# Two MLPs of a decoder trunk: one block fewer in seven products, sums moved later, transposes in two PSUM pools

## The chip, the cores and the metric

The kernel runs on one core of one Trainium2 chip. The metric is the device time in microseconds (us) of one execution, the median over several runs. One execution was also profiled; all rows below are of that one. TensorE multiplies (PE in the rows, PEld its weight loads), VectorE (DVE) and ScalarE (ACT) prepare its operands, and SyncE (SP) issues the loads.

## The reference, cut to what matters

Two residual layers over 256 tokens of width 2048, in float32: a differential attention layer, then a Mamba-2 layer, each followed by the same dense MLP with hidden width 8192:

```
def sq_relu_mlp(h, w1, w2):
    return jnp.square(jax.nn.relu(h @ w1)) @ w2
...
h = h + sq_relu_mlp(rms_norm(h, mlp_norm[i]), mlp_w1[i], mlp_w2[i])
```

The change touches only `h @ w1` and the squared ReLU after it, in both layers.

## The kernel before

Every matrix product is made from float32 numbers split in two parts: `split_weights` has ACT copy a 128x1024 piece of weights to the rounded high part (line 158) and then DVE subtract to get the low part (line 159). TensorE computes high by high, high by low and low by high. The weights come by DMA into 5 buffers (`raw`), the split pieces stand in 4 (`w`).

The hidden width is cut into eight blocks of 1024 (0 to 7), with the kinds in `MLP_KINDS`. A block of kind `s` ("plain") is `blocks`: eight groups of 128 columns, each in two steps of 8 k-tiles. One step (`wide_steps`) takes one piece of weights, 8 matmuls of 512 columns (line 169) and 8 of 256 (line 173), so a plain block has 16 steps and 16 pieces. `add_sums` (line 222) closes each group.

A block of kind `S` is `seven`: Strassen's scheme in its Winograd form over 2x2 quarters, with seven products P1 to P7 instead of eight. Each product is accumulated over four steps (i = 0 to 3); one step (`product`, lines 557 and 559) is 6 matmuls of 512 columns on one split piece of weights. That is 28 steps and 28 split pieces, and 16 additions of weights on DVE (lines 569, 579, 584, 600) that make the pieces which are sums of quarters. Seven sums of 128x512 on DVE (lines 587 to 591, 603 and 604, two copies on ACT) put the products together into the block's output `u`, and ACT applies ReLU and the square. `u` then stands tokens first, so `expand` transposes it on TensorE, 16 times 128x128 in four groups of four (line 656), and `split_pair` splits each group (ACT line 263, DVE line 264) into the operands `act` for the second matrix.

The second matrix is worked in four quarters q = 0 to 3, each of 32 token steps (`token_steps`, 12 matmuls of 512 columns on one split piece, lines 238 and 240). While quarter q runs, `both(q + 1)` makes blocks 2q+2 and 2q+3, and is advanced by `rate` steps per token step. So an MLP is: a first stage in which block 0 and block 1 alternate; q = 0 with blocks 2, 3; q = 1 with blocks 4, 5; q = 2 with blocks 6, 7; q = 3 with token steps alone. At the start of each quarter `expand` is queued for the two blocks just made (`side.add`); side work moves on by one `yield` at each `side.tick()`.

PSUM has three pools: `aux` (3 buffers: products of `seven`, and transposes), `aux1` (1: the product `p3`), and `mm` through `bank()` (4: token steps take two, a plain step's group one). Instructions of an engine run in the order in which a scheduler put them when the program was built; TensorE's is not exactly the order of the code.

Of the kernel before, what the change touches and what calls it, by code (L numbers as in the profile page):

```python
# [34 lines left out]
MASKED = -1.0e30  # L35


MLP_KINDS = "sSSSSSSS"


C_MIX0, C_MLP0, C_MIX1, C_MLP1 = 0, 16, 32, 48
# [50 lines left out]
def trunk_kernel(ctx: ExitStack, tc: tile.TileContext, x, xt, par, rope, qk, wv, wo, w10, w10s, w20, win, wdt, wout, w11, w11s, w21, out):  # L92
# [25 lines left out]
    def aux():  # L118
        return ps.tile([P, 512], F32, tag="aux", bufs=3, name="aux")
# [427 lines left out]
    def seven(pool, src, sas, u):  # L547


        a = [None] * 4  # L550

        def product(pp, which, w, i):
            for j, wj in enumerate(w):
                for kp in range(2):
                    ah, al = sas[2 * i + kp][which]
                    m = wj[:, kp * NB:(kp + 1) * NB]
                    PE.matmul(pp, lhsT=ah, rhs=m, start=(i + kp + j == 0), stop=(i == 3 and kp + j == 2))  # L557
                    if j == 0:
                        PE.matmul(pp, lhsT=al, rhs=m, start=False, stop=False)  # L559

        A11, S4, A12, S1, S3, S2, A22 = range(7)
        p1, p5 = aux(), aux()
        for i in range(4):
            while len(sas) < 2 * i + 2:
                side.tick()
            b11, b12 = load(src[0, i]), load(src[1, i])
            a[i] = pool.tile([P, 1024], F32, tag="wsum", bufs=4, name="wsum")
            w = split_weights(b11)
            V.tensor_tensor(out=a[i], in0=b11, in1=b12, op=ALU.subtract)  # L569
            product(p1, A11, w, i)  # L570
            yield
            product(p5, S1, split_weights(a[i]), i)
            yield
        S.copy(out=u[:, 0, 0], in_=p1)
        S.copy(out=u[:, 1, 1], in_=p5)
        p7, p3, p6 = aux(), aux1(), aux()
        for i in range(4):
            b12, b22 = load(src[1, i]), load(src[2, i])
            V.tensor_tensor(out=b12, in0=b22, in1=b12, op=ALU.subtract)  # L579
            product(p7, S3, split_weights(b12), i)  # L580
            yield
            product(p3, S4, split_weights(b22), i)
            yield
            V.tensor_tensor(out=a[i], in0=b22, in1=a[i], op=ALU.add)
            product(p6, S2, split_weights(a[i]), i)
            yield
        V.tensor_tensor(out=u[:, 0, 1], in0=p6, in1=u[:, 0, 0], op=ALU.add)
        V.tensor_tensor(out=u[:, 1, 0], in0=p7, in1=u[:, 0, 1], op=ALU.add)
        V.tensor_tensor(out=u[:, 0, 1], in0=u[:, 0, 1], in1=u[:, 1, 1], op=ALU.subtract)
        V.tensor_tensor(out=u[:, 0, 1], in0=p3, in1=u[:, 0, 1], op=ALU.add)  # L590
        V.tensor_tensor(out=u[:, 1, 1], in0=u[:, 1, 0], in1=u[:, 1, 1], op=ALU.subtract)
        for t in range(2):
            S.activation(u[:, t, 1], u[:, t, 1], AF.Relu)
            S.activation(u[:, t, 1], u[:, t, 1], AF.Square)
        p2, p4 = aux(), aux()
        for i in range(4):
            b21 = load(src[3, i])
            product(p2, A12, split_weights(b21), i)
            yield
            V.tensor_tensor(out=a[i], in0=a[i], in1=b21, op=ALU.subtract)  # L600
            product(p4, A22, split_weights(a[i]), i)
            yield
        V.tensor_tensor(out=u[:, 0, 0], in0=p2, in1=u[:, 0, 0], op=ALU.add)
        V.tensor_tensor(out=u[:, 1, 0], in0=u[:, 1, 0], in1=p4, op=ALU.subtract)
        for t in range(2):
            S.activation(u[:, t, 0], u[:, t, 0], AF.Relu)
            S.activation(u[:, t, 0], u[:, t, 0], AF.Square)
        yield

    def mlp(xs, w1, w1s, w2, pool, after):  # L610
# [29 lines left out]
        def expand(c, hid, place=None):  # L640
# [8 lines left out]
            for j in range(0, 4, 2):  # L649
                axs = []  # L650
                for i in range(2):
                    ax = aux().rearrange("p (a b) -> p a b", a=2)
                    for f in range(2):
                        for t in range(2):
                            c = T * (j + i) + P * f
                            PE.transpose(ax[:, f, t * P:(t + 1) * P], uf[:, t, c:c + P], ident)
                    axs.append(ax)
                for ax in axs:
                    hid += split_pair(ax, place)
                    yield  # L660

        def both(q, share):

            if not share:
                yield from hidden(2 * q)
# [7 lines left out]
            for _ in a:  # L673
                due += share
                yield
                while due >= 1:
                    due -= 1
                    next(b, None)
                    yield
            yield from b  # L680

        last = None
        side.add(sums_of(), slow=True)
        for _ in both(0, 28 / 12 if kinds[:2] == "sS" else 1.0):
            pass
        norm_mean()
        V.reciprocal(out=r2, in_=ms)
        for q in range(4):
            if q < 3:
                hid = []  # L690
                for c in (2 * q, 2 * q + 1):
                    side.add(expand(c, hid))
            else:
                hid = last
# [382 lines left out]
```

## Time and profile before

| | us |
|---|---|
| median of 3 runs | 2449.77 (2448.08 to 2452.68) |
| the profiled execution, its own time | 2449.62 |
| its span in the profile | 2447.9 |
| TensorE busy | 2434.1 |
| VectorE busy | 2098.2 |
| ScalarE busy | 1535.6 |

The span is the time from the first to the last instruction of the trace; 1.7 us of the execution lie around it. A matmul's row shows its duration with its latency, and the next one starts before it ends. So what a matmul costs is read from the starts of the rows, and a wait of TensorE is a start that comes later than the start before it plus that cost.

### The profile page before, as it was taken

To read this page: it belongs to the slowest core of one execution; us is meant where nothing else is said; L and a number is where in the kernel's file an instruction comes from. 1 tells how busy PE (TensorE), PEld (TensorE's weight loads), DVE (VectorE), ACT (ScalarE), POOL (GpSimd) and SP (SyncE) were. 2 spreads that over 40 slices of the span, in tenths; PEclk is the share of its full clock that TensorE was granted. 3 is DMA by queue.
4 is the path that set the end of the run, shared out by engine and by line. 5 is a ranking of instruction groups with operands and counts; after the bars stand their busy time and mean duration, and the time that the engine had idled before them with its cause. 6 is when DMAs were issued, how large, how long until landed. Compare 5 with 4: busy or idle time off the path is not lost.

```text
span 2447.9 us, 32626 instructions
## 1 busy us (share of the span) xinstructions
PE 2434.1 (99%) x12050; PEld 2038.8 (83%) x12050; DVE 2098.2 (86%) x2591; ACT 1535.6 (63%) x2154; POOL 1.2 (0%) x8
## 2 busy tenths in 40 slices
PE   9999999999999999999999999999999999999999
PEld 8888888878888788888888888888887888878887
DVE  6988879999998999568886887887899999899964
ACT  7666656666666666456776575775666666666653
POOL 0000000000000000000000000000000000000000
PEclk9999999999999999999999999999999999999999
DMA  8545555667667676556565556556566766776764
GB/s 287 164 157 175 167 175 194 208 232 243 230 208 230 221 231 218 191 177 211 190 198 196 174 198 199 166 189 191 190 218 220 239 229 203 238 232 206 233 205 147
DMA packets 140192, 500.54 MB, mean 204 GB/s; under 512 B 15648, under 2 KB 15840, under 8 KB 140032
## 3 DMA queue, kind: packets, MB, share of 16 engines
q1 hardware_dynamic: 137312, 489.75, 61.3%
q10 hardware_dynamic: 2720, 8.71, 1.0%
q8 instruction: 94, 1.54, 0.2%
q14 instruction: 66, 0.54, 0.1%
HBM read 496.24 MB, written 2.16 MB: 204 GB/s over the span
## 4 chain that ended last, share of the span: by engine, by line
PE 70%; DVE 18%; DMA 7%; issue 4%; ACT 1%; DVEq 0%; SPq 0%; ACTq 0%
PE pp L238 21%; PE pp L169 16%; DVE w L159 11%; PE pp L240 10%; PE pp L173 9%; PE aux L557 6%; DMA raw<-in_w11s 3%; DMA raw<-in_w10s 3%; PE aux L559 3%; DVE wsum L569 1%; DVE wsum L600 1%; DVE raw L579 1%; PE aux L878 1%; DVE h L716 1%; ACT w L158 1%
## 5 line engine op out<-in xcount | busy, mean ns | idle before, releaser
L159 DVE TENSOR_TENSOR w<-raw,w 128x1024 fp32r<-128x1024 f32 x858 | 1034.6, 1219 | 196.1 <-ACT w L158 193.5
L158 ACT CAST w<-raw 128x1024 fp32r<-128x1024 f32 x858 | 892.7, 1052 | 493.4 <-PE pp L238 316.3
L238 PE MATMUL pp<-w,act 128*128 128x512 f32 x3072 | 983.1, 391 | 0.7 <-ACT w L158 0.7
L238 PEld LDWEIGHTS pp<-w,act 128*128 128x128 f32 x3072 | 575.4, 188 | 121.7 <-ACT w L158 1.5
L240 PE MATMUL pp<-w,act 128*128 128x512 f32 x1536 | 598.5, 390 | 0.0
L169 PE MATMUL pp<-act,w 128*128 128x512 f32 x2000 | 489.0, 392 | 0.0
L169 PEld LDWEIGHTS pp<-act,w 128*128 128x128 f32 x2000 | 366.4, 188 | 72.6 <-issue 1.0
L240 PEld LDWEIGHTS pp<-w,act 128*128 128x128 f32 x1536 | 288.3, 188 | 58.0
L557 PE MATMUL aux<-w,sa 128*128 128x512 f32 x896 | 300.3, 392 | 5.2 <-DVE act L264 1.7
L173 PEld LDWEIGHTS pp<-act,w 128*128 128x128 f32 x2000 | 258.3, 191 | 11.0 <-issue 0.9
L173 PE MATMUL pp<-act,w 128*128 128x256 f32 x2000 | 266.8, 284 | 0.0
L158 ACT CAST w<-wsum 128x1024 fp32r<-128x1024 f32 x168 | 176.9, 1053 | 114.6 <-PE pp L238 43.8
L557 PE MATMUL aux<-w,act 128*128 128x512 f32 x672 | 228.8, 394 | 0.8 <-ACT w L158 0.3
L159 DVE TENSOR_TENSOR w<-wsum,w 128x1024 fp32r<-128x1024 f32 x168 | 204.8, 1219 | 1.9 <-ACT w L158 1.5
L557 PEld LDWEIGHTS aux<-w,sa 128*128 128x128 f32 x896 | 167.4, 188 | 44.3 <-DVE w L159 4.7
L559 PE MATMUL aux<-w,sa 128*128 128x512 f32 x448 | 175.2, 391 | 0.0
L557 PEld LDWEIGHTS aux<-w,act 128*128 128x128 f32 x672 | 124.8, 188 | 32.2 <-DVE w L159 6.2
L559 PE MATMUL aux<-w,act 128*128 128x512 f32 x336 | 131.4, 391 | 0.0
L559 PEld LDWEIGHTS aux<-w,sa 128*128 128x128 f32 x448 | 84.2, 188 | 16.7
L569 DVE TENSOR_TENSOR wsum<-raw 128x1024 f32<-128x1024 f32 x56 | 68.4, 1222 | 21.4 <-DMA raw<-in_w10s 11.5
L579 DVE TENSOR_TENSOR raw<-raw 128x1024 f32<-128x1024 f32 x56 | 68.5, 1222 | 20.4 <-DMA raw<-in_w11s 11.4
L600 DVE TENSOR_TENSOR wsum<-wsum,raw 128x1024 f32<-128x1024 f32 x56 | 68.0, 1220 | 7.4 <-DMA raw<-in_w11s 3.9
(218 smaller groups left out, 1736.0 us busy)
## 6 DMA issues: line engine op xcount, KB each, us to landing
raw<-in_w SPq DMA_DIRECT2D x288, 512.0 KB, 4.4
raw<-in_win SPq DMA_DIRECT2D x160, 512.0 KB, 4.1
raw<-in_w10s SPq DMA_DIRECT2D x140, 512.0 KB, 4.3
raw<-in_w11s SPq DMA_DIRECT2D x140, 512.0 KB, 4.3
raw<-in_wout SPq DMA_DIRECT2D x64, 512.0 KB, 4.1
raw<-in_qk SPq DMA_DIRECT2D x56, 512.0 KB, 4.3
raw<-in_wv SPq DMA_DIRECT2D x32, 512.0 KB, 4.2
raw<-in_wo SPq DMA_DIRECT2D x32, 512.0 KB, 4.2
```

Of the source, the lines that this page charges most:

```text
L158: S.copy(out=wh[:, s], in_=raw[:, s])
L159: V.tensor_tensor(out=wl[:, s], in0=raw[:, s], in1=wh[:, s].bitcast(F32), op=ALU.subtract)
L169: PE.matmul(acc, lhsT=wk, rhs=acts[k0 + k], start=(start and k == 0), stop=False)
L173: PE.matmul(acc[:, 0, :], lhsT=wk, rhs=acts[k0 + k][:, 0, :], start=False, stop=(stop and k == 7))
L238: PE.matmul(pp[t], lhsT=act[:, 0, tok], rhs=m, start=(s + i + k == 0), stop=(s == n - 1 and i + k == 2))
L240: PE.matmul(pp[t], lhsT=act[:, 1, tok], rhs=m, start=False, stop=False)
L557: PE.matmul(pp, lhsT=ah, rhs=m, start=(i + kp + j == 0), stop=(i == 3 and kp + j == 2))
L559: PE.matmul(pp, lhsT=al, rhs=m, start=False, stop=False)
L569: V.tensor_tensor(out=a[i], in0=b11, in1=b12, op=ALU.subtract)
L579: V.tensor_tensor(out=b12, in0=b22, in1=b12, op=ALU.subtract)
L600: V.tensor_tensor(out=a[i], in0=a[i], in1=b21, op=ALU.subtract)
L716: V.scalar_tensor_tensor(out=h[:, t, cols(j)], in0=pp[t], scalar=r2[:, t:t + 1], in1=h[:, t, cols(j)], op0=ALU.mult, op1=ALU.add)
```

## The change

- `MLP_KINDS`: block 4 becomes plain, so six of eight blocks are made with seven products. In both layers.
- In `seven`, each round of the second group of products goes P3, P7, P6 (before: P7, P3, P6), and the additions for P7 and P6 stand together ahead of P7. In the first group, the addition for P5 stands behind P1's step.
- Of the seven sums, the last three of the second group (`u4`, `c12`, `c22`, with their ReLU and square) are moved into the steps of the third group, one per step ("late"); P2's sum goes ahead of the block's end.
- The splits of block 0 are queued before the last steps of block 1 (`early`), not behind them.
- In `expand`, the second of two groups of transposes takes a buffer of the `mm` pool, not of `aux` (except for the last quarter).

```diff
-MLP_KINDS = "sSSSSSSS"
+MLP_KINDS = "sSSSsSSS"
...
             w = split_weights(b11)
+            product(p1, A11, w, i)
+            yield
             V.tensor_tensor(out=a[i], in0=b11, in1=b12, op=ALU.subtract)
-            product(p1, A11, w, i)
-            yield
             product(p5, S1, split_weights(a[i]), i)
...
         for i in range(4):
-            b12, b22 = load(src[1, i]), load(src[2, i])
+            b22, b12 = load(src[2, i]), load(src[1, i])
+            product(p3, S4, split_weights(b22), i)
+            yield
             V.tensor_tensor(out=b12, in0=b22, in1=b12, op=ALU.subtract)
+            V.tensor_tensor(out=a[i], in0=b22, in1=a[i], op=ALU.add)
             product(p7, S3, split_weights(b12), i)
             yield
-            product(p3, S4, split_weights(b22), i)
-            yield
-            V.tensor_tensor(out=a[i], in0=b22, in1=a[i], op=ALU.add)
             product(p6, S2, split_weights(a[i]), i)
             yield
...
+        late = [u4, c12, c22]
         p2, p4 = aux(), aux()
         for i in range(4):
...
             product(p4, A22, split_weights(a[i]), i)
-            yield
-        V.tensor_tensor(out=u[:, 0, 0], in0=p2, in1=u[:, 0, 0], op=ALU.add)
+            if i < 3:
+                late[i]()
+            else:
+                V.tensor_tensor(out=u[:, 0, 0], in0=p2, in1=u[:, 0, 0], op=ALU.add)
+                relu2(0, 0)
+            yield
         V.tensor_tensor(out=u[:, 1, 0], in0=u[:, 1, 0], in1=p4, op=ALU.subtract)
...
-                    ax = aux().rearrange("p (a b) -> p a b", a=2)
+                    ax = aux().rearrange("p (a b) -> p a b", a=2) if i == 0 or place is not None else bank()
...
+            side.add(early)
             yield from b
...
-        for _ in both(0, 28 / 12 if kinds[:2] == "sS" else 1.0):
+        for _ in both(0, 28 / 12 if kinds[:2] == "sS" else 1.0, expand(0, hid)):
             pass
...
-            if q < 3:
+            if q == 0:
+                side.add(expand(1, hid))
+            elif q < 3:
```

Three places show how the instructions now stand. The first is TensorE at the start of q = 1 in the first MLP, behind the last token step of q = 0; line 656 is the transposes (line 669 in the change), 557 and 559 the products, 169 and 173 plain steps. Before:

```order
L238 MATMUL pp<-w,act 128x512 x4
L557 MATMUL aux<-w,act 128x512
L559 MATMUL aux<-w,act 128x512
L557 MATMUL aux<-w,act 128x512
L559 MATMUL aux<-w,act 128x512
L557 MATMUL aux<-w,act 128x512 x2
L656 MATMUL aux<-ident,u 128x128 x8
```

The change:

```order
L238 MATMUL pp<-w,act 128x512 x4
L169 MATMUL pp<-act,w 128x512 x4
L669 MATMUL aux<-ident,u 128x128 x4
L669 MATMUL pp<-ident,u 128x128 x4
L169 MATMUL pp<-act,w 128x512 x4
L173 MATMUL pp<-act,w 128x256 x8
L669 MATMUL aux<-ident,u 128x128 x4
L669 MATMUL pp<-ident,u 128x128 x4
L169 MATMUL pp<-act,w 128x512 x4
```

The products of block 4 are gone from here; all eight groups of transposes stand between the matmuls of the first two plain steps, half of them in `aux` and half in `mm` (named pp).

The second place is TensorE at the start of q = 2 in the first MLP, with the numbers of the buffers' tiles. Before, aux_7151 is P1 of block 6, aux_7152 its P5, and aux_7168 and aux_7173 are transposes of block 4:

```order
L557 MATMUL aux_7151<-w_7158,act_3507 128x512
L656 MATMUL aux_7168<-ident_71,u_5852 128x128 x4
L656 MATMUL aux_7173<-ident_71,u_5852 128x128 x4
L557 MATMUL aux_7151<-w_7198,act_3594 128x512
...
L238 MATMUL pp_7222<-w_7225,act_7178 128x512
L557 MATMUL aux_7152<-w_7181,sa_3784 128x512
```

In the change aux_7183 is P1 and aux_7184 P5 of block 6, and aux_7250 and pp_7255 are transposes of block 5:

```order
L557 MATMUL aux_7183<-w_7190,act_3507 128x512
L557 MATMUL aux_7184<-w_7203,sa_3784 128x512
...
L238 MATMUL pp_7232<-w_7236,act_7199 128x512
L240 MATMUL pp_7232<-w_7236,act_7199 128x512
...
L669 MATMUL aux_7250<-ident_71,u_6461 128x128 x4
L669 MATMUL pp_7255<-ident_71,u_6461 128x128 x4
```

P5 has moved ahead of the first transposes, which take one buffer of `aux` and not two.

The third place is VectorE where the first stage ends and q = 0 begins, in the first MLP. u_3951 is block 1's output, u_3753 block 0's; w_4552 is the split piece for the last step of P4 of block 1, w_4582 for the first step of P1 of block 2, and w_4595 for its P5, made from the addition wsum_4581. Before:

```order
L159 TENSOR_TENSOR w_4552<-wsum_4104,w_4552 128x1024
L222 TENSOR_TENSOR u_3753<-pp_4466,u_3753 128x256
L687 RECIPROCAL r2_3752<-ms_103 128x2
L159 TENSOR_TENSOR w_4582<-raw_4577,w_4582 128x1024
L569 TENSOR_TENSOR wsum_4581<-raw_4577,raw_4579 128x1024
L603 TENSOR_TENSOR u_3951<-aux_4409,u_3951 128x512
L604 TENSOR_TENSOR u_3951<-u_3951,aux_4410 128x512
L264 TENSOR_TENSOR act_4592<-u_3753,act_4592 128x2x256
L159 TENSOR_TENSOR w_4595<-wsum_4581,w_4595 128x1024
```

The change:

```order
L264 TENSOR_TENSOR act_4591<-u_3753,act_4591 128x2x256
L159 TENSOR_TENSOR w_4552<-wsum_4104,w_4552 128x1024
L222 TENSOR_TENSOR u_3753<-pp_4460,u_3753 128x256
L159 TENSOR_TENSOR w_4582<-raw_4577,w_4582 128x1024
L616 TENSOR_TENSOR u_3951<-aux_4402,u_3951 128x512
L571 TENSOR_TENSOR wsum_4581<-raw_4577,raw_4579 128x1024
L619 TENSOR_TENSOR u_3951<-u_3951,aux_4403 128x512
L264 TENSOR_TENSOR act_4604<-u_3753,act_4604 128x2x256
L159 TENSOR_TENSOR w_4595<-wsum_4581,w_4595 128x1024
```

One split of block 0 (line 264) and P2's sum (line 603, now 616) have moved ahead of the addition for P5 (line 569, now 571).

## Rows read from the trace of the kernel before

**Rows 1.** Page, part 1: each engine's busy us (share of span) and instructions.

```profile
PE 2434.1 (99%) x12050; PEld 2038.8 (83%) x12050; DVE 2098.2 (86%) x2591; ACT 1535.6 (63%) x2154; POOL 1.2 (0%) x8
```

**Rows 2.** Timeline, TensorE, q = 3: start, us, engine, line, what, count.

```profile
2390.86 1.30 PE L238 MATMUL pp<-w,act 128*128 128x512 f32 x5
...
2393.58 1.30 PE L238 MATMUL pp<-w,act 128*128 128x512 f32 x5
```

**Rows 3.** Timeline, TensorE, first stage of the first MLP.

```profile
415.77 2.00 PE L169 MATMUL pp<-act,w 128*128 128x512 f32 x8
...
418.56 0.40 PE L557 MATMUL aux<-w,act 128*128 128x512 f32 x1
...
419.95 0.39 PE L557 MATMUL aux<-w,sa 128*128 128x512 f32 x1
...
421.31 1.98 PE L169 MATMUL pp<-act,w 128*128 128x512 f32 x8
```

**Rows 4.** Timeline, TensorE, a group of four transposes and what follows.

```profile
498.37 0.60 PE L656 MATMUL aux<-ident,u 128*128 128x128 f32 x4
498.73 0.48 PE L238 MATMUL pp<-w,act 128*128 128x512 f32 x1
```

**Rows 5.** Windows of both MLPs: length; busy us (instructions) by engine; clock, DMA.

```profile
403.70:1087.80 684.10, 680.79 (x3113) 561.42 (x3112) 607.64 (x614) 425.77 (x493) 0.00 (x0) 1.00 0.67 219
1760.60:2443.45 682.85, 678.60 (x3089) 558.47 (x3088) 598.87 (x600) 413.12 (x466) 0.00 (x0) 1.00 0.66 216
```

**Rows 6.** Windows: start of q = 0, of q = 1, the rest of q = 1, start of q = 2; both MLPs.

```profile
483.81:510.00 26.19, 24.90 (x115) 19.35 (x114) 25.89 (x30) 18.87 (x25) 0.00 (x0) 1.00 0.65 225
...
655.00:680.00 25.00, 24.50 (x123) 19.70 (x122) 23.44 (x25) 15.90 (x20) 0.00 (x0) 1.00 0.65 219
680.00:826.00 146.00, 145.81 (x640) 119.41 (x639) 134.29 (x127) 90.66 (x98) 0.00 (x0) 1.00 0.70 226
826.00:850.00 24.00, 22.81 (x117) 18.54 (x116) 22.45 (x25) 15.83 (x20) 0.00 (x0) 1.00 0.66 207
...
1842.05:1868.00 25.95, 24.53 (x112) 18.99 (x112) 25.42 (x30) 18.92 (x26) 0.00 (x0) 1.00 0.66 226
...
2013.00:2038.00 25.00, 24.52 (x123) 19.71 (x122) 23.38 (x25) 15.69 (x21) 0.00 (x0) 1.00 0.68 220
2038.00:2185.00 147.00, 146.82 (x642) 119.50 (x641) 134.56 (x128) 90.89 (x98) 0.00 (x0) 1.00 0.68 225
2185.00:2208.00 23.00, 22.46 (x114) 18.27 (x114) 22.19 (x25) 15.62 (x20) 0.00 (x0) 1.00 0.66 212
```

**Rows 7.** Timeline at the start of q = 2, first MLP; in brackets idle time and its releaser.

```profile
829.24 0.62 PE L238 MATMUL pp<-w,act 128*128 128x512 f32 x2
...
830.32 1.28 DVE L264 TENSOR_TENSOR act<-aux,act 128x512 fp32r<-128x512 f32 x2
...
831.05 0.50 PE L557 MATMUL aux<-w,sa 128*128 128x512 f32 x1 [1.19 <-DVE act L264]
```

**Rows 8.** Timeline, TensorE, at the start of q = 1, first MLP.

```profile
673.24 0.39 PE L240 MATMUL pp<-w,act 128*128 128x512 f32 x1
674.07 0.66 PE L656 MATMUL aux<-ident,u 128*128 128x128 f32 x4 [0.44 <-DVE act L264]
```

**Rows 9.** Timeline at the start of q = 0, first MLP.

```profile
487.78 1.22 DVE L569 TENSOR_TENSOR wsum<-raw 128x1024 f32<-128x1024 f32 x1
...
489.09 1.05 ACT L158 CAST w<-wsum 128x1024 fp32r<-128x1024 f32 x1 [0.43 <-DVE wsum L569]
...
490.19 0.51 PE L557 MATMUL aux<-w,sa 128*128 128x512 f32 x1 [0.76 <-DVE u L604]
...
491.77 0.33 PE L656 MATMUL aux<-ident,u 128*128 128x128 f32 x1 [0.36 <-ACT u L607]
```

**Rows 10.** Page, part 5: groups; count, busy, mean ns, idle before and its releaser.

```profile
L159 DVE TENSOR_TENSOR w<-raw,w 128x1024 fp32r<-128x1024 f32 x858 | 1034.6, 1219 | 196.1 <-ACT w L158 193.5
...
L569 DVE TENSOR_TENSOR wsum<-raw 128x1024 f32<-128x1024 f32 x56 | 68.4, 1222 | 21.4 <-DMA raw<-in_w10s 11.5
```

More of the change, by code (lines that the diff above doesn't have):

```diff
@@ L568, in seven @@
             w = split_weights(b11)
-            V.tensor_tensor(out=a[i], in0=b11, in1=b12, op=ALU.subtract)
             product(p1, A11, w, i)
             yield
+            V.tensor_tensor(out=a[i], in0=b11, in1=b12, op=ALU.subtract)
             product(p5, S1, split_weights(a[i]), i)
@@ L588, in seven, with relu2, u4, c12 @@
         V.tensor_tensor(out=u[:, 1, 0], in0=p7, in1=u[:, 0, 1], op=ALU.add)
[L589 to L594, printed above, removed]
+        def relu2(t, n):
+            S.activation(u[:, t, n], u[:, t, n], AF.Relu)
+            S.activation(u[:, t, n], u[:, t, n], AF.Square)
+        def u4():
+            V.tensor_tensor(out=u[:, 0, 1], in0=u[:, 0, 1], in1=u[:, 1, 1], op=ALU.subtract)
+        def c12():
+            V.tensor_tensor(out=u[:, 0, 1], in0=p3, in1=u[:, 0, 1], op=ALU.add)
+            relu2(0, 1)
+        def c22():
+            V.tensor_tensor(out=u[:, 1, 1], in0=u[:, 1, 0], in1=u[:, 1, 1], op=ALU.subtract)
+            relu2(1, 1)
+        late = [u4, c12, c22]
         p2, p4 = aux(), aux()
@@ L601, in seven @@
             product(p4, A22, split_weights(a[i]), i)
+            if i < 3:
[3 more added lines that the diff above has]
+                relu2(0, 0)
             yield
-        V.tensor_tensor(out=u[:, 0, 0], in0=p2, in1=u[:, 0, 0], op=ALU.add)
         V.tensor_tensor(out=u[:, 1, 0], in0=u[:, 1, 0], in1=p4, op=ALU.subtract)
-        for t in range(2):
-            S.activation(u[:, t, 0], u[:, t, 0], AF.Relu)
-            S.activation(u[:, t, 0], u[:, t, 0], AF.Square)
+        relu2(1, 0)
         yield
@@ L660, in expand, with both @@
                     yield
-        def both(q, share):
+        def both(q, share, early=None):
             if not share:
@@ L683, in mlp @@
         side.add(sums_of(), slow=True)
-        for _ in both(0, 28 / 12 if kinds[:2] == "sS" else 1.0):
+        hid = []
+        for _ in both(0, 28 / 12 if kinds[:2] == "sS" else 1.0, expand(0, hid)):
             pass
```

## The prediction

> **What bounds the kernel now.** I read the page's first part, then the timeline of TensorE for the price of each kind of matmul, then windows with their counts, and last the timeline where TensorE is late. TensorE is busy 99% of the span [rows 1], but busy time of pipelined matmuls says little, so I price the starts. In the last quarter one token step of 12 matmuls begins 2.72 us after the other [rows 2]: 0.2267 us per matmul of 512 columns with nothing in its way. A plain step takes 418.56 - 415.77 = 2.79 us; a product step takes 1.39 us when its stationary operand is `act` and 1.36 us when it is `sa` [rows 3]. Four transposes take 0.36 us [rows 4].
>
> From the code an MLP has 1536 matmuls of token steps, 16 plain steps, 7 x 28 product steps (12 with `act`, 16 with `sa` in each block), 28 groups of four transposes, and 8 such groups (first MLP) or 2 (second) for the norm; that is 3112 and 3088 matmuls, and the windows count one more each [rows 5]. Priced: 1536 x 0.2267 = 348.2; 16 x 2.79 = 44.6; 7 x (12 x 1.39 + 16 x 1.36) = 7 x 38.4 = 269.1; 28 x 0.36 = 10.1; norm 2.9 or 0.7. That makes 674.9 and 672.7 us of work in windows of 684.10 and 682.85 us [rows 5]. So TensorE waits 9.2 + 10.2 = 19.4 us in the two MLPs together, and all else there is matmuls, one behind the other, at a granted clock of 1.00. This is all that any smoothing can give back.
>
> Where the 19.4 us lie comes from shorter windows in the same way. A window also counts the matmuls still running at its start (0.39 us long, 0.2267 apart, so 1.7); those and the transposes are taken off, and the rest priced [rows 6]:
> - start of q = 0 (16 transposes): 26.19 - 97.3 x 0.2267 - 1.4 = 2.7 us, second MLP 3.1; together 5.8.
> - start of q = 1 (32 transposes): 25.00 - 89.3 x 0.2267 - 2.9 = 1.9, and 1.9; together 3.8.
> - rest of q = 1: 146.00 - 638.3 x 0.2267 = 1.3, and 1.8; together 3.1.
> - start of q = 2 (32 transposes): 24.00 - 83.3 x 0.2267 - 2.9 = 2.2, and 1.9; together 4.1.
> - elsewhere: 19.4 - 16.8 = 2.6.
>
> **The change, part by part.** *Block 4 plain.* TensorE gets a plain block of 44.6 us for a block of seven products of 38.4 us and four groups of transposes, 1.4 us. That is +4.8 us in each MLP, **+9.6 us** in all. TensorE has no slack in which this could lie, so it counts in full. VectorE is relieved by 12 splits at 1.219 us and 16 additions at 1.222 us [rows 10], 34.2 us per MLP, ScalarE by 12 copies; four loads per MLP go. These are worth only the waits that they end.
>
> *Start of q = 1.* TensorE stands at 674.07 before a group of transposes, due at 673.24 + 0.23 = 673.47, until line 264 has split an earlier group [rows 8]: the three buffers of `aux` are full. In the change all eight groups stand here between plain steps, and half use `mm`. A plain step wants one split of VectorE in 2.79 us; a product step wants a split and 16/28 of an addition, 1.92 us, in 1.37 us. So VectorE has room for the groups' splits. I leave 0.4 us per MLP: **-3.0**. Bounds: nothing to -3.8. The buffers of `mm` that the groups take are then free only when VectorE has added the last token pair into `h`; that runs while the first plain steps do, and if it is late the next group waits in its place.
>
> *Start of q = 2.* P5 comes at 831.05; it was due at 829.24 + 2 x 0.2267 = 829.69, and was released by line 264 [rows 7]. P1 and two groups of transposes, which the scheduler put ahead of P5, held all of `aux`; P5 got its buffer when VectorE had split a group. In the change P5 stands ahead of the transposes, and these take one buffer of `aux` for each of `mm`. The cause is taken away; the work of VectorE is not: eight splits of 128x512 still come here beside additions for block 6. I leave 0.7 us per MLP: **-2.7**. Bounds: nothing to -4.1.
>
> *Rest of q = 1.* `rate` goes from 58/30 to 45/30 steps per token step. Before, VectorE has 1.22 + 1.93 x 1.92 = 4.9 us to do while TensorE does 2.72 + 1.93 x 1.37 = 5.4: 92%, which is what the window shows (134.29 of 146.00) [rows 6]. In the change it has 3.1 of 6.9 us during block 4 and 4.1 of 4.8 (86%) during block 5. I leave 0.5 us per MLP: **-2.1**. Bounds: nothing to -3.1.
>
> *Late sums, order P3 P7 P6, spread additions, elsewhere.* Outside q = 1 these only reorder the same work of VectorE; up to the first P3 of block 1 the engines' orders are the same as before. Of the 2.6 us I take **-0.4**; bounds -1.5 and, if an addition pair ahead of P7 holds up a split, +1.
>
> *Start of q = 0.* Here VectorE is busy 25.89 of 26.19 us [rows 6], so what is put ahead of something delays it. P5's weights hang on one chain: the addition begins at 487.78, ScalarE copies from 489.09, TensorE starts P5 at 490.19 after 0.76 us idle [rows 9]. The change puts one split of block 0 and P2's sum ahead of that addition, two operations of 128x512 at 0.64 us (two take 1.28 in [rows 7]): up to 1.3 us later per MLP. Queued behind P5 are P1's next step and the token steps. On the other side, behind the block's last sum only one ReLU and square stand instead of two, so the transposes that waited for line 607 at 491.77 [rows 9] come earlier. I take +0.4 per MLP, **+0.8**: bounds +2.6 (VectorE's order alone decides) and -3 (half of the 5.8 goes).
>
> **Sum.** 9.6 - 3.0 - 2.7 - 2.1 - 0.4 + 0.8 = +2.2 us. Made against the profiled execution's own 2449.6 us: 2451.8. The median of the runs, 2449.77, is 0.15 us above that execution, which changes nothing. A measurement of this kernel can tell about 0.2%, 4.9 us, from no change; +2 us is inside it. The extremes are 2449.6 + 9.6 + 2.6 = 2461.8 (nothing given back) and 2449.6 + 9.6 - 19.4 = 2439.8 (no wait left).
>
> **A rule against this reading.** By busy time alone TensorE's weight loads have 561.42 of 684.10 us in the first MLP (82%) and VectorE 607.64 (89%) [rows 5]. The Trainium skill (Perfetto Trace Analysis, Identifying the Most-Contended Engine) says not to judge TensorE by its matmul busy time but by weight loads, and to work first on the engine with the highest occupancy. By that rule VectorE is the bound, and taking 34.2 us from it should pay; this is the faster rival below. The starts of the matmuls say otherwise: in q = 1 VectorE is at 92% and TensorE waits 1% of the time.
>
> **Rivals.**
> - *Slower: the waits at the starts are VectorE's order, not PSUM's.* At the start of q = 0 both operations delay P5 in full (+2.6), and at q = 2 the splits of line 264 still stand between splits of weights, so P5's buffer comes free but its weights don't (0 instead of -2.7); of the rest of q = 1 half a microsecond per MLP comes back (-1.0), at the start of q = 1 the full -3.0. 9.6 + 2.6 - 3.0 - 1.0 = +8.2: 2457.8. For it: VectorE's 99% at q = 0, 22.45 of 24.00 us at q = 2 [rows 6]. Against it: P5 at q = 2 was released by line 264, while its high part needs only ScalarE. It decides when less than 9.6 - 4.9 = 4.7 us come back.
> - *Faster: VectorE's load is the cause of every wait.* With 34.2 us less of it in q = 1, later sums and free buffers, the 13.6 us of waits outside the start of q = 0 all but vanish (-13.0), and half of the 5.8 too (-2.9): 9.6 - 15.9 = -6.3, 2443.3. For it: three of the four releasers in [rows 7 to 9] are VectorE. Against it: q = 0 and q = 2 have the same VectorE work as before, and the first stage too. It needs 14.5 us back to show.
>
> **Chances.** Forecast (within 0.2%) 0.64; slower rival and its kin 0.22; faster 0.14. The range of 8 in 10 takes in the slower rival's price and half of the way to the faster one's: 2445.5 to 2457.5. That leaves about 1 in 10 on each side.
>
> **What the profile after would show.** Lines 169 and 173 with 128 more matmuls each per MLP, 557 and 559 with 112 and 56 fewer, transposes 96 instead of 112 per MLP. The windows of both MLPs priced as above: work 679.7 and 677.5 us, waits about 12 us together. No matmul of P5 at the start of q = 2 released by line 264; no wait of over 0.5 us at the start of q = 1; at the start of q = 0 P5 idle for 1 to 2 us instead of 0.76. VectorE's busy time about 70 us lower. The prediction is wrong if a plain step among token steps takes clearly other than 2.79 us, if the sums of waits are under 5 or over 15 us, or if anything outside the MLPs changes.

## The result and the profile after

The change makes the kernel a little slower: 2456.16 us (median of 20 runs, 2451.86 to 2460.38) against 2450.61 us (20 runs, 2448.08 to 2453.54) in the same session, a ratio of 1.0021 with a 95% interval of 1.0014 to 1.0027. That is at the 0.2% that a measurement can tell. The profiled execution took 2456.6 us (span 2454.9), 7.0 us more than that of before.

The page's first part of the kernel after, as in [rows 1]:

```profile
PE 2440.6 (99%) x12194; PEld 2052.3 (84%) x12194; DVE 2038.8 (83%) x2537; ACT 1516.4 (62%) x2142; POOL 1.2 (0%) x8
```

VectorE is relieved of 59.4 us (about 70 were forecast), and nothing of it is seen in the time. The windows of the two MLPs, which answer to [rows 5], then the start of q = 1, the rest of q = 1, the start and the rest of q = 2 in the first MLP, which answer to [rows 6]:

```profile
403.70:1091.10 687.40, 683.65 (x3186) 568.58 (x3186) 578.41 (x588) 416.28 (x487) 0.00 (x0) 1.00 0.65 215
1763.85:2450.40 686.55, 682.33 (x3162) 565.28 (x3160) 568.91 (x572) 403.18 (x460) 0.00 (x0) 1.00 0.65 212
```

```profile
655.80:680.80 25.00, 25.00 (x147) 21.91 (x146) 16.53 (x20) 13.87 (x20) 0.00 (x0) 1.00 0.52 165
680.80:829.10 148.30, 148.30 (x696) 124.39 (x695) 114.80 (x110) 84.35 (x95) 0.00 (x0) 1.00 0.66 217
829.10:854.10 25.00, 25.00 (x120) 20.87 (x119) 24.40 (x25) 16.74 (x19) 0.00 (x0) 1.00 0.69 229
854.10:1000.20 146.10, 144.61 (x651) 119.05 (x650) 132.44 (x129) 92.31 (x101) 0.00 (x0) 1.00 0.67 217
```

The MLPs are 3.30 and 3.70 us longer: all of the 7.0. The swap was priced at 9.6, so only 2.6 us of waits ended, not 7.4. In three of the four shorter windows TensorE is busy to the last hundredth; in the rest of q = 2 it is not (144.61 of 146.10).

To see where the waits are I took, from start to start of TensorE's matmuls, what each takes beyond the median of its kind in the same trace, and added it up by place, both MLPs together. (By this count before has 21.8 us of waits, against 19.4 priced by hand, after 18.0. The rows of the table add up to +6.8 us, the windows to +7.0: the count is good to some tenths.)

| us, both MLPs | before | after | difference | forecast |
|---|---|---|---|---|
| matmuls without waits (the swap) | | | +10.5 | +9.6 |
| start of q = 1 | 3.6 | 0.9 | -2.8 | -3.0 |
| rest of q = 1 | 2.9 | 0.0 | -2.8 | -2.1 |
| start of q = 2 | 4.0 | 0.3 | -3.6 | -2.7 |
| start of q = 0 | 6.3 | 5.9 | -0.4 | +0.8 |
| elsewhere: first stage | 2.7 | 1.7 | -1.0 | |
| elsewhere: rest of q = 0 | 0.8 | 2.3 | +1.6 | |
| elsewhere: rest of q = 2 | 1.4 | 6.8 | +5.4 | |
| elsewhere, sum (with q = 3) | | | +5.9 | -0.4 |

The timeline of TensorE at the start of q = 2, which answers to [rows 7]: P1's last two matmuls, then P5.

```profile
831.24 0.61 PE L557 MATMUL aux<-w,act 128*128 128x512 f32 x2
831.69 0.39 PE L557 MATMUL aux<-w,sa 128*128 128x512 f32 x1
```

P5 starts 0.45 us, two matmuls, after them, and has no idle time in brackets. At the start of q = 1 ([rows 8]) the transposes now follow half a plain step on time, with half of them in `mm`:

```profile
657.00 1.07 PE L169 MATMUL pp<-act,w 128*128 128x512 f32 x4
657.91 0.60 PE L669 MATMUL aux<-ident,u 128*128 128x128 f32 x4
658.35 0.60 PE L669 MATMUL pp<-ident,u 128*128 128x128 f32 x4
```

At the start of q = 0 ([rows 9]) the addition for P5 comes 1.09 us later than before, at 488.87, and P5 waits longer, as forecast:

```profile
488.27 0.69 DVE L616 TENSOR_TENSOR u<-aux,u 128x512 f32<-128x512 f32 x1
...
488.87 1.22 DVE L571 TENSOR_TENSOR wsum<-raw 128x1024 f32<-128x1024 f32 x1
...
490.31 1.03 ACT L158 CAST w<-wsum 128x1024 fp32r<-128x1024 f32 x1
...
491.39 0.50 PE L557 MATMUL aux<-w,sa 128*128 128x512 f32 x1 [1.47 <-ACT w L158]
```

The new waits lie in the rest of q = 2. The timeline of VectorE, TensorE and ScalarE there:

```profile
938.40 1.06 ACT L158 CAST w<-raw 128x1024 fp32r<-128x1024 f32 x1 [1.66 <-PE pp L238]
...
940.53 1.22 DVE L159 TENSOR_TENSOR w<-raw,w 128x1024 fp32r<-128x1024 f32 x1
...
940.73 2.00 ACT L158 CAST w<-raw 128x1024 fp32r<-128x1024 f32 x2 [1.27 <-DVE raw L581]
...
942.78 1.23 DVE L582 TENSOR_TENSOR wsum<-raw,wsum 128x1024 f32<-128x1024 f32 x1 [1.03 <-DMA raw<-in_w10s]
...
943.92 3.49 DVE L159 TENSOR_TENSOR w<-raw,w 128x1024 fp32r<-128x1024 f32 x3
...
944.33 0.39 PE L559 MATMUL aux<-w,sa 128*128 128x512 f32 x1
...
945.20 0.98 PE L557 MATMUL aux<-w,sa 128*128 128x512 f32 x3 [0.48 <-DVE w L159]
...
950.57 1.23 DVE L611 TENSOR_TENSOR wsum<-wsum,raw 128x1024 f32<-128x1024 f32 x1 [0.89 <-DMA raw<-in_w10s]
...
951.71 3.49 DVE L159 TENSOR_TENSOR w<-raw,w 128x1024 fp32r<-128x1024 f32 x3
...
952.99 0.96 PE L557 MATMUL aux<-w,sa 128*128 128x512 f32 x3 [0.65 <-DVE w L159]
```

The addition of line 582 (now the one for P6) stands 1.03 us before its load, with VectorE idle from 941.75. Behind it come three splits of line 159, the first of them for P3's step. ScalarE had copied the high part of that one by 939.46 (the row at 938.40) and those of the other two by 942.73, so splitting could have begun at 941.75, but VectorE took its instructions in order. The low part that TensorE needs comes at 945.15, and TensorE, due at 944.33 + 0.23, starts at 945.20: 0.64 us late. Eight microseconds on the same happens with line 611 (the addition for P4), 0.8 us late.

### The profile page after: what moved, and what is told of

Read it like the earlier page. It is cut to its first block, busy times and chain, and to the rows that moved or that the text cites. A ratio compares the mean times of both kernels' runs of the same rounds, so it can differ in the third digit from the quotient of the medians.

```text
span 2454.9 us, 32782 instructions
## 1 busy us (share of the span) xinstructions
PE 2440.6 (99%) x12194; PEld 2052.3 (84%) x12194; DVE 2038.8 (83%) x2537; ACT 1516.4 (62%) x2142; POOL 1.2 (0%) x8
## 4 chain that ended last, share of the span: by engine, by line
PE 76%; DVE 13%; DMA 5%; issue 3%; ACT 2%; DVEq 0%; SPq 0%; ACTq 0%
PE pp L238 23%; PE pp L169 19%; PE pp L240 11%; PE pp L173 10%; DVE w L159 9%; PE aux L557 6%; PE aux L559 3%; DMA raw<-in_w11s 3%; DMA raw<-in_w10s 2%; ACT w L158 1%; DVE wsum L582 1%; PE aux L895 1%; DVE raw L581 1%; PE pp L354 1%; DVE wsum L611 1%
## 5 line engine op out<-in xcount | busy, mean ns | idle before, releaser
L169 PE MATMUL pp<-act,w 128*128 128x512 f32 x2256 | 553.8, 392 | 0.0
L169 PEld LDWEIGHTS pp<-act,w 128*128 128x128 f32 x2256 | 413.3, 188 | 81.6 <-issue 1.0
L173 PEld LDWEIGHTS pp<-act,w 128*128 128x128 f32 x2256 | 293.2, 191 | 13.6 <-issue 0.9
L173 PE MATMUL pp<-act,w 128*128 128x256 f32 x2256 | 302.5, 283 | 0.0
L557 PE MATMUL aux<-w,sa 128*128 128x512 f32 x768 | 258.6, 393 | 6.8 <-DVE w L159 3.4
L158 ACT CAST w<-wsum 128x1024 fp32r<-128x1024 f32 x144 | 151.5, 1052 | 107.7 <-PE pp L238 54.2
L557 PE MATMUL aux<-w,act 128*128 128x512 f32 x576 | 194.3, 390 | 0.4 <-DVE u L587 0.4
L159 DVE TENSOR_TENSOR w<-wsum,w 128x1024 fp32r<-128x1024 f32 x144 | 175.7, 1220 | 6.7 <-ACT w L158 6.0
L557 PEld LDWEIGHTS aux<-w,sa 128*128 128x128 f32 x768 | 142.9, 188 | 43.4 <-DVE w L159 9.5
L559 PE MATMUL aux<-w,sa 128*128 128x512 f32 x384 | 149.7, 390 | 0.0
L559 PE MATMUL aux<-w,act 128*128 128x512 f32 x288 | 112.3, 390 | 0.0
L559 PEld LDWEIGHTS aux<-w,sa 128*128 128x128 f32 x384 | 72.1, 188 | 14.5
L221 ACT COPY u<-pp 128x256 f32<-128x256 f32 x80 | 29.2, 372 | 70.0 <-PE pp L173 69.9
L820 DVE SCALAR_TENSOR_TENSOR cy<-u,cwb,cy 128x256 f32<-128x256 f32 x144 | 63.6, 482 | 9.9 <-ACT cy L818 9.5
```

What stands on the lines that cost most here:

```text
L158: S.copy(out=wh[:, s], in_=raw[:, s])
L159: V.tensor_tensor(out=wl[:, s], in0=raw[:, s], in1=wh[:, s].bitcast(F32), op=ALU.subtract)
L169: PE.matmul(acc, lhsT=wk, rhs=acts[k0 + k], start=(start and k == 0), stop=False)
L173: PE.matmul(acc[:, 0, :], lhsT=wk, rhs=acts[k0 + k][:, 0, :], start=False, stop=(stop and k == 7))
L221: S.copy(out=dst[:, t, :], in_=pp[t][:, 1, :])
L820: V.scalar_tensor_tensor(out=y[:, i, :], in0=u[:, i, k:k + T], scalar=cwb[:, w + k:w + k + 1], in1=y[:, i, :], op0=ALU.mult, op1=ALU.add)
```

## The experiments

Each kernel was compared with runs of before on its own chip (medians of before 2448.23, 2448.37 and 2448.83 us in the three groups). "Late" is the sum over both MLPs, worked out as above; the first stage is left out. The rows before and after of the table are profiles of the first session, where before took 2450.61 us. In the three groups, about 2 us faster, before was not profiled, so small differences between these two rows and the others may be the session's.

| kernel | ratio (95%) | start q0 | rest q0 | q1 | start q2 | rest q2 |
|---|---|---|---|---|---|---|
| before | 1 | 6.3 | 0.8 | 6.5 | 4.0 | 1.4 |
| after | 1.0021 (1.0014 to 1.0027) | 5.9 | 2.3 | 0.9 | 0.3 | 6.8 |
| x_swap | 0.9994 (0.9985 to 1.0002) | 4.1 | -0.4 | 1.7 | 2.1 | 0.6 |
| x_noswap | 1.0023 (1.0014 to 1.0032) | 6.5 | 3.5 | 1.0 | 3.9 | 8.3 |
| x_oldorder | 1.0007 (0.9998 to 1.0016) | 5.5 | 2.2 | 1.1 | 0.3 | 0.6 |
| x_noload | 0.9994 (0.9985 to 1.0003) | 5.9 | -0.1 | 0.9 | 0.3 | 0.6 |
| y_pairs | 1.0003 (0.9994 to 1.0011) | 7.1 | -0.3 | 1.5 | 0.3 | 1.0 |
| z_apart | 1.0024 (1.0015 to 1.0033) | 5.6 | 1.1 | 0.9 | 0.3 | 7.5 |
| y_oldfirst | 0.9995 (0.9986 to 1.0004) | 6.2 | -0.4 | 0.9 | 0.3 | 1.3 |
| y_noearly | 1.0007 (0.9998 to 1.0015) | 6.2 | 3.2 | 0.9 | 0.3 | 0.6 |
| r6_after | 1.0022 (1.0013 to 1.0031) | 6.6 | -0.4 | 0.9 | 0.3 | 3.0 |
| p3late | 1.0027 (1.0017 to 1.0038) | 5.7 | 2.3 | 0.9 | 0.3 | 8.3 |
| r6_oldfirst | 1.0054 (1.0041 to 1.0066) | 7.3 | 0.7 | 1.6 | 0.3 | 5.9 |
| r6_swap | 1.0059 (1.0046 to 1.0072) | 9.4 | 0.6 | 1.8 | 2.8 | 5.5 |

**The swap, the edits, and the order P3 first.** Theory A: the swap costs about what was forecast, and the waits in the rest of q = 2 come from the edits in `seven`, above all from P3 ahead of P7. Its rival B: the swap itself moves them there. x_swap is the kernel before with block 4 plain and nothing else:

```diff
-MLP_KINDS = "sSSSSSSS"
+MLP_KINDS = "sSSSsSSS"
```

> The kernel before with block 4 plain and no other edit. Theory A (the new order P3, P7, P6 with its two additions side by side makes VectorE's low parts late in q = 0 and q = 2; the swap itself costs 9.6 us and ends the waits of q = 1): before +3 to +6 us; in the profile the waits at the start of q = 1 and in the rest of q = 1 are gone (-5 to -6 us), those at the start of q = 2 stand (about 4), and the rest of q = 2 waits no more than in the kernel before (about 1.4 us in both MLPs). Theory B (the swap shifts the steps so that q = 2 runs badly; the other edits are innocent): before +8 to +11 us, with 5 to 7 us of waits in the rest of q = 2.

Measured: 2446.85 us, 0.9994. The rest of q = 2 has 0.6 us of waits: B falls. The time is under what either theory forecast, so the swap is even cheaper than A said: its price is in the trace (matmuls without waits +9.9 us), but the waits in q = 1 and q = 2 fall from 11.9 to 4.4 us by it alone. That leaves +2.4 us; the runs show -1.4 (-3.7 to +0.5). Up to q = 1 of the first MLP TensorE's and VectorE's instructions stand in the order of before, so what differs there is hardly the swap's doing.

x_noswap is the kernel after with seven blocks of eight in seven products:

> The changed kernel with seven of eight blocks in seven products, so all edits but the swap. Theory A: the waits at the starts of q = 1 and q = 2 are mostly gone (-4 to -6), but the new order adds waits in the rest of q = 0, q = 1 and q = 2 (+5 to +9): before -2 to +4 us. Theory B: only the gains: before -4 to -8 us.

Measured: 2453.81 us, 1.0023. The edits without the swap are as slow as the whole change, with 8.3 us in the rest of q = 2. That is 5.6 us over before, more than the -2 to +4 that A gave them.

x_oldorder takes only the second group of products back to the order of before:

```diff
-            b22, b12 = load(src[2, i]), load(src[1, i])
-            product(p3, S4, split_weights(b22), i)
-            yield
+            b12, b22 = load(src[1, i]), load(src[2, i])
             V.tensor_tensor(out=b12, in0=b22, in1=b12, op=ALU.subtract)
-            V.tensor_tensor(out=a[i], in0=b22, in1=a[i], op=ALU.add)
             product(p7, S3, split_weights(b12), i)
             yield
+            product(p3, S4, split_weights(b22), i)
+            yield
+            V.tensor_tensor(out=a[i], in0=b22, in1=a[i], op=ALU.add)
```

> The changed kernel with the second group of products in its former order (P7, P3, P6, loads and additions as before). Theory A: the waits in the rest of q = 0 and q = 2 fall from about 9 us (both MLPs) to 2 to 3, so 5 to 7 us under the changed kernel, level with the kernel before. Theory B: as the changed kernel within 2 us, the waits in q = 2 unchanged.

Measured: 2449.54 us, 1.0007; 0.6 us in the rest of q = 2, and with the rest of q = 0 together 2.8, as A said. By the ratios it is 3.4 us under the changed kernel, less than A's 5 to 7. The waits of VectorE in this stretch of the first MLP (waiting tile and line, us in total, times, longest), after first, then x_oldorder:

```profile
DVE w L159 <- ACT w L158: 5.6, 5, 1.5
DVE wsum L582 <- DMA raw<-in_w10s: 3.2, 4, 1.1
DVE wsum L611 <- DMA raw<-in_w10s: 3.0, 2, 2.2
```

```profile
DVE w L159 <- ACT w L158: 7.8, 9, 1.5
DVE wsum L611 <- DMA raw<-in_w10s: 1.0, 1, 1.0
DVE wsum L571 <- DMA raw<-in_w10s: 0.7, 1, 0.7
```

With P7 first no addition of the second group waits for a load here. The order of VectorE's instructions tells why. In the changed kernel, at the place of the timeline above (wsum_7879 and wsum_7920 are P6's additions of rounds 2 and 3, raw_8083 and raw_8133 `b22`, raw_8085 and raw_8135 `b12`; DMAHW is the semaphore of a load):

```
999 L581 TENSOR_TENSOR raw_8085<-raw_8083,raw_8085 128x1024 [waits DMAHW4_49,DVE_49]
1000 L159 TENSOR_TENSOR w_8068<-raw_8066,w_8068 128x1024 [waits DMAHW2_49,Activation_49]
1001 L582 TENSOR_TENSOR wsum_7920<-raw_8133,wsum_7920 128x1024 [waits DMAHW6_49]
1002 L159 TENSOR_TENSOR w_8087<-raw_8083,w_8087 128x1024 [waits Activation_49]
1003 L159 TENSOR_TENSOR w_8098<-raw_8085,w_8098 128x1024 [waits Activation_49]
```

and in x_oldorder (raw_8083 and raw_8133 are `b12` here, the others `b22`):

```
1003 L159 TENSOR_TENSOR w_8108<-raw_8106,w_8108 128x1024 [waits DMAHW5_49,Activation_49]
1004 L579 TENSOR_TENSOR raw_8133<-raw_8135,raw_8133 128x1024 [waits DMAHW7_49,DMAHW6_49]
1005 L584 TENSOR_TENSOR wsum_7920<-raw_8135,wsum_7920 128x1024
```

P6's addition needs `b22` alone. With P3 first `b22` is loaded first, and the scheduler put the addition of round 3 at that load's arrival, ahead of the splits of round 2 for P3 and P7 (w_8087, w_8098). These are the splits that come late in the timeline. With P7 first its addition has waited for both loads, and P6's, behind it, waits for none. Over the whole program 40 of the 48 additions for P6 wait for a load in the changed kernel, none in x_oldorder and none in before.

x_noload is the kernel after without the second load of `b12`; the subtraction for P7 reads the tile `a[i]` instead, so it computes other sums with the same instructions:

```diff
-            b22, b12 = load(src[2, i]), load(src[1, i])
+            b22 = load(src[2, i])
+            b12 = wp.tile([P, 1024], F32, tag="raw", bufs=5, name="raw")
...
-            V.tensor_tensor(out=b12, in0=b22, in1=b12, op=ALU.subtract)
+            V.tensor_tensor(out=b12, in0=b22, in1=a[i], op=ALU.subtract)
```

> The changed kernel without the second load of the quarter b12: the subtraction for P7 reads the piece a in its place, so P7 to P2 get other numbers; the buffer, the additions and the splits stay. If VectorE is late in q = 2 because an addition waits for that load, the waits in the rest of q = 2 fall to 2 us or less and the time to 3 to 6 us under the changed kernel. If VectorE's own work in the new order is the cause, the waits stay at 6 to 7 us and the time is that of the changed kernel within 2 us.

Measured: 2446.62 us, 0.9994, with 0.6 us in the rest of q = 2 and none in the rest of q = 0. P3 stands first here too, but there is no second load, the subtraction comes first, and none of P6's additions waits for a load. So the order of the products costs nothing that shows when there is no second load. The kernel moves 471 MB in place of 496, but its other loads are no faster for it: for the weights of the blocks in seven products (`in_w10s`, `in_w11s`) the median from issue to landing is 4.2 us, in the changed kernel 4.3.

**Which of the edits.** z_apart keeps P3 first, but puts the addition for P6 behind P7's step again:

```diff
-            V.tensor_tensor(out=a[i], in0=b22, in1=a[i], op=ALU.add)
             product(p7, S3, split_weights(b12), i)
             yield
+            V.tensor_tensor(out=a[i], in0=b22, in1=a[i], op=ALU.add)
             product(p6, S2, split_weights(a[i]), i)
```

> The changed kernel with P3 still first, but the addition for P6 back behind P7's step, so the two additions are apart. If it is the two additions side by side that make VectorE stand before loads, the waits in the rest of q = 0 and q = 2 fall to 2 to 3 us (both MLPs) and the time by 4 to 6 us under the changed kernel. If it is P3 ahead of P7 (one raw buffer held for a step more), the waits stay at 6 to 9 us and the time within 2 us of the changed kernel.

Measured: 2453.82 us, 1.0024; 7.5 us in the rest of q = 2. So it is P3 ahead of P7, not the two additions side by side, as the second half of the forecast has it: moved in the code, P6's addition was put by the scheduler where it stood in after, 40 of 48 waiting for a load.

y_oldfirst is x_oldorder with the first group taken back too (the addition for P5 ahead of P1's step); late sums, early splits and transposes in two pools stay:

```diff
             w = split_weights(b11)
+            V.tensor_tensor(out=a[i], in0=b11, in1=b12, op=ALU.subtract)
             product(p1, A11, w, i)
             yield
-            V.tensor_tensor(out=a[i], in0=b11, in1=b12, op=ALU.subtract)
```

> The changed kernel with both groups of products as before (second group P7, P3, P6; addition for P5 ahead of P1's step); swap, late sums, early split and pairs stay. If the later addition for P5 causes the waits of P5 in q = 0 (2.2 us in the rest of q = 0, 5.4 us at its start, with the second group's order alone restored), these fall by 2 to 4 us and the time is 3 to 5 us under the kernel before. If the early split and the late sums cause them, they stay and the time is level with the kernel before.

Measured: 2447.39 us, 0.9995; the waits in the rest of q = 0 are gone (2.2 in x_oldorder). Between x_oldorder and y_oldfirst lie 0.0012, 2.9 us, though their intervals touch. But the time is level with before, not 3 to 5 us under it, and the start of q = 0 has 6.2 us where x_oldorder has 5.5, so the later addition is not what makes the waits of that place as a whole. Nor is it enough for those in the rest of q = 0: x_noload has the later addition too, and has none.

y_noearly is x_oldorder without `early`: the splits of block 0 are queued behind block 1 again.

```diff
-            side.add(early)
```

> The changed kernel with the second group's order as before and without the early split of block 0. If the split ahead of P5's addition is what delays P5 at the start of q = 0, the waits there fall from 5.4 us (both MLPs) to 3 to 4, the rest of q = 0 stays at 2.2, and the time is 1 to 2 us under that with the order alone restored. If not, nothing moves by more than 0.5 us.

Measured: 2449.90 us, 1.0007. The waits do not fall, they are 0.7 us more at the start of q = 0 and 1.0 more in the rest (3.2). The early splits were not the cause.

y_pairs is x_swap with the transposes in two pools and no other edit:

```diff
-                    ax = aux().rearrange("p (a b) -> p a b", a=2)
+                    ax = aux().rearrange("p (a b) -> p a b", a=2) if i == 0 or place is not None else bank()
```

> The kernel before with block 4 plain and the second group of transposes in the mm pool, nothing else. If PSUM's aux buffers cause the waits at the start of q = 2, these fall from the 2.1 us of the swap alone (both MLPs) to about 0.3, and the time to 3 us (2 to 5) under the kernel before. If VectorE's order is the cause (the slower rival), the waits at the start of q = 2 stay at about 2 us and the time is that of the swap alone, 1 to 2 us under the kernel before.

Measured: 2448.96 us, 1.0003. The start of q = 2 falls from 2.1 us to 0.3, as the forecast's reading (buffers of PSUM) says; the start of q = 0 shows 7.1 against 4.1, and no time is gained, where 2 to 5 us were forecast.

**Buffers for the loads.** Another reason was thinkable: with P3 first, `b22` and `b12` hold their buffers longer, and the five `raw` buffers run short. Then a sixth should help, and so should a later load of `b12`. r6_after is the kernel after with six buffers; to make room, the small tiles of the sums of activations take a `raw` buffer instead of their own:

```diff
-        raw = wp.tile([P, 1024], F32, tag="raw", bufs=5, name="raw")
+        raw = wp.tile([P, 1024], F32, tag="raw", bufs=6, name="raw")
...
-        a = pool.tile([P, 2, T], F32, tag="relu", bufs=2, name="a")
+        af = wp.tile([P, 1024], F32, tag="raw", bufs=6, name="raw")
+        a = af[:, 0:512].rearrange("p (a b) -> p a b", a=2)
```

> The changed kernel with six raw buffers for loads instead of five (room is made by putting the two small tiles of the sums of activations into one raw buffer, in the first stage). If the new order makes VectorE's additions stand before loads because too few raw buffers are free, the waits in the rest of q = 0 and q = 2 fall from 9.2 us (both MLPs) to 2 or less, and the time to 5 to 8 us under the changed kernel. If the additions' place in VectorE's order is the cause whatever the loads do, the waits stay at 6 or more and the time within 2 us of the changed kernel.

Measured: 2454.47 us, 1.0022. The waits in the rests of q = 0 and q = 2 fall from 9.1 to 2.5 us in its profile, but 1.9 us come up in the first stage, and the median is that of after. (The profiled execution, 2451.52 us, was one of its fastest.) In it 30 of the 48 additions for P6 wait for a load, not 40, so its order changed with the buffers, and the fall does not tell the two apart. Neither of the two forecasts came out.

p3late loads `b12` behind P3's step:

```diff
-            b22, b12 = load(src[2, i]), load(src[1, i])
+            b22 = load(src[2, i])
             product(p3, S4, split_weights(b22), i)
             yield
+            b12 = load(src[1, i])
```

> The changed kernel with the load of b12 moved behind P3's step. If b12, loaded one step before it is used, only holds a raw buffer idle, this frees it and the waits in the rest of q = 0 and q = 2 fall from 9.2 us to 3 to 5. If that load is wanted early and comes too late already, they rise to 12 or more and the time goes 2 to 6 us over the changed kernel.

Measured: 2456.58 us, 1.0027; 2.2 us in the rest of q = 2 of the first MLP, 6.1 of the second. With 2.3 us in the rest of q = 0 that makes 10.6, between the two forecasts. It does not help: `b12` idle in its buffer is not the cause. In this kernel 44 of the 48 additions wait for a load.

r6_oldfirst and r6_swap have the same six buffers in y_oldfirst and in x_swap.

> Block 4 plain, late sums, early split and pairs, both groups of products in their former order, and six raw buffers. Against the same kernel with five buffers (0.9995 of the kernel before) what is left of waits lies at the start of q = 0 (6.2 us in both MLPs). If loads hold these up, they fall to 3 or less and the time to 3 to 5 us under the kernel before; if VectorE's work does, they stay and the time is 1 to 2 us under it.

> The kernel before with block 4 plain and six raw buffers, nothing else. The swap alone is at 0.9994 of the kernel before with 8.5 us of waits in both MLPs, 4.1 of them at the start of q = 0 and 2.1 at the start of q = 2. The 2.1 are of PSUM's aux buffers and stay; if loads make the 4.1, 1 to 3 us come back. So 2 to 5 us under the kernel before; the same as the swap alone if loads have no part in it.

Measured: 2462.80 and 2463.98 us, 1.0054 and 1.0059, where all that was forecast lay under before. Both are clearly slower than with five buffers, with 6.3 and 6.8 us late in the first stage alone. The waits of TensorE's weight loads in r6_swap:

```profile
PEld aux L558 <- ACT w L158: 11.2, 12, 2.7
PEld aux L558 <- DVE w L159: 10.3, 21, 1.3
```

and in x_swap, where line 557 is the same product:

```profile
PEld aux L557 <- ACT w L158: 1.6, 4, 0.5
```

Copies of ScalarE and splits of VectorE both come late. In the rest of q = 2 VectorE stands before loads; in r6_oldfirst, first MLP:

```profile
DVE raw L580 <- DMA raw<-in_w10s: 4.2, 4, 1.4
DVE wsum L570 <- DMA raw<-in_w10s: 3.1, 3, 1.4
DVE wsum L612 <- DMA raw<-in_w10s: 2.2, 2, 1.2
```

These are the additions for P7, P5 and P4. Additions for P6 that wait for a load are not it, there are none in either kernel.

A part of r6_swap's time is TensorE's clock. In both MLPs TensorE stood idle at the start of q = 0 (2.28 and 2.29 us), and the granted clock then was 0.50 of full speed in one stretch (1.2 GHz, not 2.4), where matmuls of 512 columns start 0.42 us apart, not 0.23. In the first MLP (rows of the timeline, then the window):

```profile
493.77 0.50 PE L558 MATMUL aux<-w,sa 128*128 128x512 f32 x1 [2.28 <-ACT w L158]
...
494.50 0.63 PE L558 MATMUL aux<-w,sa 128*128 128x512 f32 x1
494.92 0.63 PE L560 MATMUL aux<-w,sa 128*128 128x512 f32 x1
```

```profile
494.14:497.55 3.41, 3.41 (x10) 2.65 (x9) 3.41 (x4) 2.46 (x4) 0.00 (x0) 0.50 0.94 382
```

Two such stretches at half speed cost some 3.4 us (an estimate, half of their length) of the 16 us by which r6_swap's ratio lies above x_swap's. The profile of r6_oldfirst has no such stretch, so the clock is not what makes six buffers slow. Whether the sixth buffer does it, or the sums' tiles in it, or the order that the scheduler makes of both, these runs don't tell.

## Why the prediction came out as it did

**Right: what bounds the kernel, and the swap's price.** TensorE's matmuls stand one behind the other at a granted clock of 1.00, and the plain block costs +10.5 us (+9.6 forecast). That VectorE's relief is worth only the waits it ends held too: x_swap takes 16 additions and 12 splits per MLP off VectorE and ends waits worth about the swap's price, no more. The faster rival (-6.3 us) is outside x_swap's interval (-3.7 to +0.5). The Trainium skill (Perfetto Trace Analysis, Identifying the Most-Contended Engine) advises to work first on the engine of highest occupancy. By [rows 5] that would have been VectorE; it went down by 59 us in the change and by 60 in x_swap, and no gain over the price of the swap came of it.

**Right: the starts of q = 1 and q = 2 and the rest of q = 1,** -9.2 us against -7.8. Their causes are less single than I wrote. In q = 1 either half is enough: 1.7 us are left with the swap alone, 1.0 with the edits alone. At the start of q = 2 neither is: 2.1 with the swap alone, 3.9 with the edits alone, 0.3 with both. Without the swap there are eight groups of transposes there, and P5 is on time as forecast, but later groups of transposes wait for line 264 in its place (0.45 and 0.52 us in the first MLP of x_noswap): the second pool alone does not suffice for eight. With four groups it does end the wait (y_pairs).

**Start of q = 0:** P5 is idle for 1.47 us in the first MLP, as forecast (1 to 2), released by the copy that follows the later addition. But the place as a whole has the 6 us of before (-0.4 for +0.8): what comes sooner made up for it. The slower rival (2457.8) came close in time by another way: the waits that it kept at q = 2 are gone, and it did not have those that came.

**The step that failed** is "Late sums, order P3 P7 P6, spread additions, elsewhere": -0.4 us with a bound of +1, measured +5.9. The bound had a pair of additions holding up a split; z_apart shows that it is not the pair. I argued that outside q = 1 these "only reorder the same work of VectorE". What a reorder moves is not only work but what VectorE stands in front of. An addition that stands before a load makes everything behind it on VectorE wait, the splits too whose inputs are there (1.03 us in the timeline above). Of the bundle, late sums, early splits and transposes cost nothing that shows (y_oldfirst 0.9995, x_swap 0.9994). The order P3 first costs 1.0021 - 1.0007, 3.4 us, in the rest of q = 2 (these two intervals touch; the groups of kernels below are clearer); with P5's addition behind P1's step go 2.9 us, in the rest of q = 0. With the -1.2 us of y_oldfirst that makes +5.1, and measured were +5.5 (medians). I had also written that waits of over 15 us would prove the forecast wrong; they are 16.8 by its own method. That the time was still inside the range was luck: the range held the slower rival, and what filled it was neither the forecast's mechanism nor that rival's.

This can be read over the kernels: the additions for P6 that wait for a load by the order of instructions, VectorE's waits for loads in the rest of q = 2 of the first MLP, and how late TensorE is there.

| | x_oldorder | x_swap | y_oldfirst | x_noload | before | after | r6_after | p3late | z_apart | r6_swap | x_noswap | r6_oldfirst |
|---|---|---|---|---|---|---|---|---|---|---|---|---|
| P6's additions that wait for a load | 0 of 48 | 0 of 48 | 0 of 48 | 0 of 48 | 0 of 56 | 40 of 48 | 30 of 48 | 44 of 48 | 40 of 48 | 0 of 48 | 48 of 56 | 0 of 48 |
| VectorE for loads, us | 1.7 | 3.1 | 3.9 | 4.0 | 4.9 | 7.1 | 7.3 | 7.6 | 8.0 | 8.2 | 9.1 | 9.5 |
| TensorE late, us | 0.3 | 0.3 | 0.3 | 0.3 | 0.6 | 2.7 | 1.9 | 2.2 | 3.3 | 3.7 | 4.3 | 4.7 |

In these profiles, one execution each, VectorE absorbs up to about 5 us of standing before loads; what it stands beyond that, TensorE loses about one for one. The second MLP shows the same (before 5.2 and 0.8 us, after 8.8 and 4.1). The two kernels with six buffers and the old order lie on the same line with no addition for P6 waiting. So the standing is what tells, whichever addition does it. Of the 5.4 us by which after stands longer than x_oldorder, 3.2 are at the additions for P6 (line 582) and 2.0 at those for P4 (line 611).

Shown is that the order P3 first costs the time: the five kernels that have it with its second load take 1.0021 to 1.0027, the six with five buffers that lack one of the two 0.9994 to 1.0007. Shown is also that P6's additions then stand before loads where they did not. That the scheduler's place for them is the only cause is argued: a kernel with P3 first and P6's addition held back behind the splits was not run.

**Open:** why P5's addition behind P1's step costs 2.9 us in the rest of q = 0, if it does (in x_noload it does not); why a sixth buffer slows the old order, in the first stage above all; and the 4 us or more at the start of q = 0, which every version has.

## What to carry to other kernels

An order is judged by what each in-order engine will stand in front of, not by how much work it has: look at what waits for a load, and what ready work is queued behind it. When one engine has no gaps, a relief of another is worth the waits that it ends, to be added up by place before and not as a share of busy time. Time each edit of a bundle by itself: here the parts that moved transposes and sums cost nothing that shows, and two reorders of loads and additions cost it all, as far as the runs part them.

## What the runs showed that I had not expected

- Up to q = 1, x_swap has the same order of TensorE's instructions as before in the first MLP, yet one execution of it had 2.0 us of waits up to there and one of before 4.2. The two were taken in different sessions. Single profiles differ by microseconds, and small terms need the runs.
- A sixth `raw` buffer, with small tiles moved into it, cost 0.6% (x_swap 2446.85, r6_swap 2463.98 us).
